# Attention halves of the third block emitted in 18 steps between linear matmuls, and spatial gating behind the second half's query, key and value linears

## The chip, the cores and the metric

The kernel runs on one core of a Trainium2 chip. The metric is the time of one execution on the device in microseconds (us), as the median of several runs. A second, separate execution is taken by the hardware profiler; its trace gives the durations of single instructions.

## The reference, cut to what matters

The model is three blocks in a row on 512 tokens of width 1024. The change touches the third block alone, between the normalisation of its input and the projection of its merged output:

```python
h = rms_norm_3(x, mix_norm[l])
z = h @ w_in[l]
g_a, g_b, z_uv, z_q, z_k, z_v = jnp.split(z, COL_SPLITS, axis=-1)
y_a = gmlp_chunk_mixer(z_uv, a_ln_gain[l], a_ln_bias[l], a_w_s[l], a_b_s[l])
...
y_b = diff_attention(q, k, v, positions, ...)
m = jax.nn.sigmoid(g_a) * (y_a @ a_w_proj[l]) + jax.nn.sigmoid(g_b) * (y_b @ b_w_proj[l])
x = x + m @ w_out[l]
```

The first branch is a gated mixer, the second a differential attention, in which each head subtracts one softmax from another:

```python
def gmlp_chunk_mixer(z_uv, ln_g, ln_b, w_s, b_s):
    z = jax.nn.gelu(z_uv, approximate=False)
    u, v = jnp.split(z, 2, axis=-1)
    v = layer_norm(v, ln_g, ln_b)
    vc = v.reshape(bsz, seq // CHUNK_3, CHUNK_3, A_GROUPS, A_GROUP_DIM)
    w = jnp.where(causal[None], w_s, jnp.zeros_like(w_s))
    f = jnp.einsum('gts,bcsge->bctge', w, vc) + b_s.T[:, :, None]
    return u * f.reshape(bsz, seq, A_WIDTH)

...
s = jnp.einsum('bhmqd,bhmkd->bhmqk', qb, kf)
p = jax.nn.softmax(jnp.where(mask, s, -jnp.inf), axis=-1)
a = p[:, :, 0] - lam * p[:, :, 1]
return jnp.einsum('bhqk,bhkd->bhqd', a, vf)
```

The last lines stand in `diff_attention`, behind the norm and the rotary turn of q and k; its output is normalised for each head after them.

## The kernel before

**Linears.** All activations stand in SBUF in tiles of 128 x 512. A linear is written as three matmuls for each product, high weight by high input, high weight by low input, low weight by high input. Weights come by DMA from the SP queue (line 236), ScalarE rounds them to the high part (line 218, `split`), VectorE subtracts that for the low part (line 219), 1024 columns at a time. `lin_fm` gives its output feature-major: matmuls of 512 columns (lines 248 to 250, called by line 261) into one bank. `lin_tm` gives it token-major: two halves of 256 output columns, each of 96 matmuls of 256 columns (lines 277 to 279) into two banks.

**PSUM banks.** The names of tiles in the trace tell the pool. `pl` has two banks and stays for the whole kernel (`ps_lin`). `pa` has two (`ps`), `pq` two pairs (`ps_pair`, the scores). `env.banks()` closes the pool of pa and pq and opens a new one. Line 269 toggles `self.bank` at each half of a `lin_tm`, and line 270 takes pa or pl by it.

**The third block.** Attention is done in two halves of four heads. The order in which the work is written is: query, key and value linears of the first half (`qk_half`, `v_half`); its attention `attend(0)`; the linear of u (feature-major, gelu in line 1885) and of v of the gating (token-major, gelu in line 1893 and a layer norm of each 128 tokens up to line 1905); the spatial gating (64 matmuls of line 1913, the gate in lines 1915 to 1918 and a split); `finish(o0)`, which turns the four outputs of the half (line 1858) and splits them; query, key and value of the second half; `attend(1)`; the gates of the first branch with their projections (`gated`, 288 matmuls in lines 248 to 250); `finish(o1)`; the gates of the second branch.

`qk_half` copies the linear's output, squares and sums it, applies the rotary turn (lines 1767 to 1772), takes a root (lines 204 to 213) and scales each 128 tokens (line 1778). Then 16 transposes by TensorE into four pa tiles (line 1783) and a copy of each by ScalarE (line 1785) turn it. `attend` has 16 heads' parts, one for each of four query tiles `b` and four heads. Each is a chain over four engines: scores in a pq pair (line 108), maximum and two exponentials (lines 1826 and 1827), reciprocal, scaling, subtraction, up to four transposes (line 1836), a copy, up to four product matmuls (line 1842) and a copy (line 1843). After four heads `safe_norm` normalises the output tile (up to line 1809).

**What sets the order.** Each engine runs its own queue strictly in order. A scheduler fixes these queues when the kernel is built: of the instructions that are ready by its cost model it takes the one written first, unless a priority is raised. So where attention is written ahead of a linear, the linear's matmuls fill what attention leaves, and what is written in a mixed order comes out mixed.

Of the kernel before, what the change touches and what calls it, by code (L numbers as in the profile page):

```python
# [17 lines left out]
ALU = mybir.AluOpType  # L18
PSUM = bass.MemoryType.PSUM

P = 128
S = 512
D = 1024
NC4 = S // P
# [9 lines left out]
class Env:  # L34
# [5 lines left out]
    def __init__(self, tc, ctx, n_long=33, n_tmp=6, n_scan=8, n_out=4):  # L40
# [12 lines left out]
        self.stream, self.bank = "", 0  # L53

# [197 lines left out]
    def lin_fm(self, w, c0, ncols, h, epi, k0=0, nk=KB, ready=()):  # L252
# [3 lines left out]
        for t in range(ncols // P):  # L256
            ps = self.ps_lin()
            for ka, kb in zip(cuts, cuts[1:]):
                wh, wl = ready[t] if t < len(ready) else self.weights(w, k0 + ka, kb - ka, c0 + t * P, P)
                for k in range(ka, kb):  # L260
                    self.mm3(ps, wh[:, k - ka, :], wl[:, k - ka, :], h[0][k], h[1][k], k == 0, k == nk - 1)
            epi(t, ps)

    def lin_tm(self, w, c0, h, epi, ncols=S):
# [3 lines left out]
        for g in range(ncols // n):  # L268
            self.bank = 1 - self.bank
            banks = [(self.ps, self.ps_lin)[self.bank]() for _ in range(2)]  # L270
            ps = [banks[c // 2][:, (c % 2) * n:(c % 2 + 1) * n] for c in range(NC4)]
            for ka in range(0, KB, 4):
                wh, wl = self.weights(w, ka, 4, c0 + g * n, n)
                for k in range(ka, ka + 4):
                    for c in range(NC4):
# [3 lines left out]
                        mm(ps[c], h[0][k][:, tok], wl[:, k - ka, :], start=False, stop=k == KB - 1 and c % 2 == 1)  # L279
            for c in range(NC4):  # L280
                epi(c, g, ps[c])
# [1379 lines left out]
def third_block(env, a, x):  # L1661
# [153 lines left out]
    def attend(half, qf, kf, vt):  # L1815

        outs = []

        def head(b, hd, o):
# [12 lines left out]
            nc.vector.scalar_tensor_tensor(ex[0][:, :n], ex[0][:, :n], st[:, 6:7], ex[1][:, :n], ALU.mult, ALU.subtract)  # L1832
            with env.on(""):
                ps = env.ps()
            for s in range(b + 1):
                nc.tensor.transpose(H(ps, s), H(ex[0], s), env.ident)  # L1836
            pt = env.tmp()
            nc.scalar.copy(pt[:, :n], ps[:, :n])
# [4 lines left out]
            nc.scalar.copy(H(o, hd), po[:, :P])  # L1843

        for b in range(NC4):
            o = env.out()
            for hd in range(4):
                with env.on("ab"[hd % 2]):
                    head(b, hd, o)
            safe_norm(o)  # L1850
            outs.append(o)
        return outs
# [25 lines left out]
    env.banks()  # L1878
# [28 lines left out]
    ya = ([], [])  # L1907
    for pair in range(4):
        ps = env.ps()
        for c in range(NC4):  # L1910
            for e in range(2):
                g = 2 * pair + e
                mm(ps[e * 64:(e + 1) * 64, c * P:(c + 1) * P], vg[c][:, g * 64:(g + 1) * 64], H(wt[g // 4], g % 4), start=True, stop=True)
        t = env.tmp()
        c4 = lambda v: v.rearrange("p (c i) -> p c i", c=4)
        nc.vector.tensor_tensor(c4(t), c4(ps), H(bs, pair)[:, None, :].to_broadcast([P, 4, P]), ALU.add)
        nc.vector.tensor_tensor(ut[pair], t, ut[pair], ALU.mult)
        hi, lo = env.parts(ut[pair])
        ya[0].append(hi)
        ya[1].append(lo)  # L1920

# [66 lines left out]
```

## Time and profile before

| | |
|---|---|
| median of 3 runs | 2968.88 us (2967.75 to 2970.56) |
| profiled execution | 2967.77 us, span 2966.0 us |
| TensorE (PE) busy | 2880.2 us, 97% |
| VectorE (DVE) busy | 1723.3 us, 58% |
| ScalarE (ACT) busy | 1107.8 us, 37% |
| mean granted TensorE clock | 0.987 |

PE is TensorE's matmuls, PEld its weight loads, DVE is VectorE, ACT is ScalarE, SP issues DMAs. The span is the time from the first to the last instruction in the trace, 1.8 us less than that execution's own time. Busy shares are means over the span: a stage can stand beside them that is quite different. A row of a timeline gives start, duration, engine, line, operation, output and inputs with sizes, how many alike, and in brackets how long the engine was idle before and for whom it waited. Matmuls overlap, so that the distance of two starts is the pace, not the duration. The granted clock is given as a share of 2.4 GHz.

### The profile page before, as it was taken

The numbers are of one execution on the slowest core, as the hardware profiler recorded it, in microseconds if no ns is written. First come the engines' busy times: TensorE is split into PE (matmuls) and PEld (weight loads), VectorE is DVE, ScalarE is ACT, GpSimd is POOL, SyncE is SP. The second block draws the span as 40 slices with busy tenths as digits, with TensorE's granted clock in tenths as the row PEclk, the third lists the DMA queues.
The fourth block names the chain that finished last, engine by engine and source line by source line (L and its number), as shares of the span: only waits on it lengthen the run. The fifth ranks groups of instructions, "written<-read, shape, count | busy, mean of one in ns | idle before, by whom it ended". The sixth has DMA issues, their size and how long they took to land. (4 is left out here: it accounts for less than half of the span.)

```text
span 2966.0 us, 38950 instructions
## 1 busy us (share of the span) xinstructions
PE 2880.2 (97%) x14919; PEld 2380.8 (80%) x14919; DVE 1723.3 (58%) x3936; ACT 1107.8 (37%) x2086; POOL 47.5 (2%) x99
## 2 busy tenths in 40 slices
PE   7999999999999999989999999999999999999999
PEld 5878888888788886777878878888887978878887
DVE  7787737655655357987653563433667573554333
ACT  5435424433322234322353342222455562332221
POOL 1000000000000000000000000000000000000000
PEclk8999999999999999989999999999999999999999
DMA  5222233233445332222113423333322214333332
GB/s 139 69 71 67 73 93 93 66 102 93 140 140 169 91 96 87 77 57 52 46 33 89 124 81 100 94 99 100 125 72 71 65 58 128 100 93 96 97 93 92
DMA packets 481642, 269.03 MB, mean 91 GB/s; under 512 B 30591, under 2 KB 469056, under 8 KB 481456
## 3 DMA queue, kind: packets, MB, share of 16 engines
q1 hardware_dynamic: 445104, 254.62, 29.7%
q10 hardware_dynamic: 34512, 10.49, 1.4%
q0 software_dynamic: 1840, 1.43, 0.6%
q8 instruction: 118, 1.93, 0.3%
q14 instruction: 68, 0.56, 0.1%
HBM read 252.20 MB, written 14.16 MB: 90 GB/s over the span
## 5 line engine op out<-in xcount | busy, mean ns | idle before, releaser
L218 ACT CAST wh<-wr 128x1024 fp32r<-128x1024 f32 (+3 forms) x447 | 454.4, 1017 | 1288.4 <-PE pl L249 901.7
L250 PE MATMUL pl<-h,wl 128*128 128x512 f32 x2216 | 876.8, 396 | 13.9 <-DVE wl L219 13.8
L248 PE MATMUL pl<-h,wh 128*128 128x512 f32 x2216 | 878.4, 396 | 6.3 <-ACT wh L218 4.2
L249 PE MATMUL pl<-h,wh 128*128 128x512 f32 x2216 | 874.9, 395 | 0.0
L219 DVE TENSOR_TENSOR wl<-wr,wh 128x1024 fp32r<-128x1024 f32 (+3 forms) x447 | 526.2, 1177 | 439.8 <-ACT wh L218 433.9
L250 PEld LDWEIGHTS pl<-h,wl 128*128 128x128 f32 x2216 | 419.4, 189 | 103.7 <-DVE wl L219 17.4
L248 PEld LDWEIGHTS pl<-h,wh 128*128 128x128 f32 x2216 | 419.7, 189 | 97.2 <-ACT wh L218 6.5
L249 PEld LDWEIGHTS pl<-h,wh 128*128 128x128 f32 x2216 | 419.3, 189 | 86.3 <-issue 3.4
L250 PE MATMUL pl<-long,wl 128*128 128x512 f32 x648 | 253.3, 391 | 0.0
L249 PE MATMUL pl<-long,wh 128*128 128x512 f32 x648 | 252.9, 390 | 0.3 <-DVE long L219 0.3
L248 PE MATMUL pl<-long,wh 128*128 128x512 f32 x648 | 252.8, 391 | 0.0
L590 DVE SCALAR_TENSOR_TENSOR long<-pl,long 128x512 f32<-128x512 f32 x72 | 49.8, 691 | 175.9 <-PE pl L250 175.9
L249 PEld LDWEIGHTS pl<-long,wh 128*128 128x128 f32 x648 | 121.7, 188 | 25.7 <-DVE long L219 0.7
L250 PEld LDWEIGHTS pl<-long,wl 128*128 128x128 f32 x648 | 121.7, 188 | 25.4 <-issue 0.8
L248 PEld LDWEIGHTS pl<-long,wh 128*128 128x128 f32 x648 | 121.7, 188 | 24.8
L578 DVE TENSOR_TENSOR tmp<-tmp,pl 128x512 f32<-128x512 f32 x66 | 45.4, 687 | 150.0 <-PE pl L250 150.0
L248 PE MATMUL pl<-tmpa,wh 128*128 128x512 f32 (+1 forms) x312 | 125.0, 401 | 4.8 <-DVE tmp L685 2.8
L249 PE MATMUL pl<-tmpb,wh 128*128 128x512 f32 (+1 forms) x312 | 124.6, 400 | 0.0
L250 PE MATMUL pl<-tmpa,wl 128*128 128x512 f32 (+1 forms) x312 | 124.0, 397 | 0.0
L248 PEld LDWEIGHTS pl<-tmpa,wh 128*128 128x128 f32 (+1 forms) x312 | 59.4, 191 | 18.7 <-ACT h L218 3.5
L250 PEld LDWEIGHTS pl<-tmpa,wl 128*128 128x128 f32 (+1 forms) x312 | 59.3, 190 | 13.8 <-issue 0.5
L249 PEld LDWEIGHTS pl<-tmpb,wh 128*128 128x128 f32 (+1 forms) x312 | 59.3, 190 | 12.7 <-issue 0.3
(781 smaller groups left out, 3947.7 us busy)
## 6 DMA issues: line engine op xcount, KB each, us to landing
wr<-in_w_in SPq DMA_DIRECT2D x169, 512.0 KB, 3.9
wr<-in_w_ffn_in SPq DMA_DIRECT2D x44, 512.0 KB, 3.9
wr<-in_ffn_w_gate SPq DMA_DIRECT2D x44, 512.0 KB, 3.8
wr<-in_ffn_w_up SPq DMA_DIRECT2D x44, 512.0 KB
wr<-in_ffn_w_down SPq DMA_DIRECT2D x32, 448.0 KB, 3.6
wr<-in_w_ada SPq DMA_DIRECT2D x24, 512.0 KB, 3.6
wr<-in_w_out SPq DMA_DIRECT2D x16, 512.0 KB, 4.1
wr<-in_ffn_w_down SPq DMA_DIRECT2D x16, 512.0 KB, 3.9
```

The costliest lines, as they stand in the source:

```text
L218: pin(self.nc.scalar.copy(hi, src))
L219: pin(self.nc.vector.tensor_tensor(lo, src, hi.bitcast(F32), ALU.subtract))
L248: mm(ps, wh, xh, start=first, stop=False)
L249: mm(ps, wh, xl, start=False, stop=False)
L250: mm(ps, wl, xh, start=False, stop=last)
L578: nc.vector.tensor_tensor(t1, t1, ps, ALU.mult)
L590: nc.vector.scalar_tensor_tensor(x[i], ps, scale, x[i], ALU.mult, ALU.add)
```

## The change

The 16 heads' parts of `attend` are cut in three works, `scores`, `turned` and `products`, and `attend` becomes a generator of 18 steps: step i emits the products of part i - 2, the transposes of part i - 1 and the scores of part i. The first step of a half is emitted at once. The others are called from inside linears: `env.weave(o0, 3)` hands the generator to `Env`, and `step` runs one of its steps after every three k steps of a `lin_fm` (nine matmuls), where a k step of a `lin_tm` (12 matmuls) counts as two. For the second half it is one step after every five k steps. `unweave` emits what is left. While a generator is handed over, `lin_tm` does not toggle the bank but holds it at 1 (pl). The first half is so emitted between the matmuls of u and v of the gating, the second between those of the first branch's gates and projections. The spatial gating and `finish` of the first half move behind the second half's query, key and value linears. No arithmetic changes.

```diff
@@ Env
+    def weave(self, side, every):
+        self.side, self.every, self.count = side, every, 0
+
+    def step(self, n=1):
+        self.count += n
+        if self.side is not None and self.count >= self.every:
+            self.count -= self.every
+            kept, self.stream = self.stream, ""
+            if next(self.side, self) is self:
+                self.side = None
+            self.stream = kept
+
+    def unweave(self):
+        for _ in self.side or ():
+            pass
+        self.side = None
@@ lin_fm
                     self.mm3(ps, wh[:, k - ka, :], wl[:, k - ka, :], h[0][k], h[1][k], k == 0, k == nk - 1)
+                    self.step()
@@ lin_tm
         for g in range(ncols // n):
-            self.bank = 1 - self.bank
+            self.bank = 1 - self.bank if self.side is None else 1
             banks = [(self.ps, self.ps_lin)[self.bank]() for _ in range(2)]
...
                         mm(ps[c], h[0][k][:, tok], wl[:, k - ka, :], start=False, stop=k == KB - 1 and c % 2 == 1)
+                    self.step(2)
@@ attend
-        def head(b, hd, o):
+        def scores(b, hd):
             n = (b + 1) * P
...
             nc.vector.scalar_tensor_tensor(ex[0][:, :n], ex[0][:, :n], st[:, 6:7], ex[1][:, :n], ALU.mult, ALU.subtract)
+            return ex[0]
+
+        def turned(b, ex):
             with env.on(""):
                 ps = env.ps()
             for s in range(b + 1):
-                nc.tensor.transpose(H(ps, s), H(ex[0], s), env.ident)
+                nc.tensor.transpose(H(ps, s), H(ex, s), env.ident)
             pt = env.tmp()
-            nc.scalar.copy(pt[:, :n], ps[:, :n])
+            nc.scalar.copy(pt[:, :(b + 1) * P], ps[:, :(b + 1) * P])
+            return pt
+
+        def products(b, hd, pt):
+            if hd == 0:
+                outs.append(env.out())
+            o = outs[b]
             with env.on(""):
                 po = env.ps()
             for s in range(b + 1):
                 mm(po[:, :P], H(pt, s), H(vt[s], hd), start=s == 0, stop=s == b)
             nc.scalar.copy(H(o, hd), po[:, :P])
-
-        for b in range(NC4):
-            o = env.out()
-            for hd in range(4):
-                with env.on("ab"[hd % 2]):
-                    head(b, hd, o)
-            safe_norm(o)
-            outs.append(o)
-        return outs
+            if hd == 3:
+                safe_norm(o)
+
+        heads = [(b, hd) for b in range(NC4) for hd in range(4)]
+        kept = {}
+        for i in range(len(heads) + 2):
+            for lag, work in ((2, products), (1, turned), (0, scores)):
+                j = i - lag
+                if 0 <= j < len(heads):
+                    b, hd = heads[j]
+                    with env.on("ab"[hd % 2]):
+                        if lag == 0:
+                            kept[j] = scores(b, hd)
+                        elif lag == 1:
+                            kept[j] = turned(b, kept[j])
+                        else:
+                            products(b, hd, kept.pop(j))
+            yield outs
@@ the order of the third block
     o0 = attend(0, qf, kf, vt)
-    env.banks()
+    a0 = next(o0)
+    env.weave(o0, 3)
...
     env.lin_tm(w_in, VG0, h, vg_epi)
-    ya = ([], [])
-    for pair in range(4):
...
+    env.unweave()
+    env.banks()
...
-    finish(o0)
     qf, kf, vt = qk_half(Q0 + S, 0), qk_half(K0 + S, 1), v_half(1)
+    ya = ([], [])
+    for pair in range(4):
...
+    finish(a0)
     env.banks()
     o1 = attend(1, qf, kf, vt)
+    a1 = next(o1)
+    env.weave(o1, 5)
+    gated(GA0, a["a_w_proj_3"][0], ya, 4, True)
+    env.unweave()
     env.banks()
-    gated(GA0, a["a_w_proj_3"][0], ya, 4, True)
-    finish(o1)
+    finish(a1)
     gated(GB0, a["b_w_proj_3"][0], yb, 8, False)
```

The change inserts lines above, so that line 1783 of before (the query's and key's transposes) is line 1806 after it, 1785 is 1808, 1778 is 1801, 277 to 279 are 299 to 301, 1893 is 1937, 1827 is 1852, 1913 is 1977. Two places show how it moves instructions.

The first place is TensorE's queue between the query and the key linear of the second half. `pa` and `pl` are banks, `h` is the input, `wh` and `wl` a weight's parts, `long` the scaled query. Before, at the first transposes of the query:

```order
L279 MATMUL pl_19807<-wl_19865,h_17578 128x256
L277 MATMUL pl_19807<-wh_19864,h_17578 128x256
L278 MATMUL pl_19807<-wh_19864,h_17579 128x256
L279 MATMUL pl_19807<-wl_19865,h_17578 128x256
L1783 MATMUL pa_19777<-ident_98,long_19530 128x128
L1783 MATMUL pa_19784<-ident_98,long_19530 128x128
L277 MATMUL pl_19806<-wh_19864,h_17584 128x256
L278 MATMUL pl_19806<-wh_19864,h_17585 128x256
L279 MATMUL pl_19806<-wl_19865,h_17584 128x256
L1783 MATMUL pa_19777<-ident_98,long_19545 128x128
```

After, first behind the query's last matmul:

```order
L300 MATMUL pl_19483<-wh_19540,h_17591 128x256
L301 MATMUL pl_19483<-wl_19541,h_17590 128x256
L1806 MATMUL pa_19669<-ident_98,long_19422 128x128
L1806 MATMUL pa_19676<-ident_98,long_19422 128x128
L1806 MATMUL pa_19669<-ident_98,long_19437 128x128
L1806 MATMUL pa_19676<-ident_98,long_19437 128x128
L1806 MATMUL pa_19669<-ident_98,long_19452 128x128
L1806 MATMUL pa_19676<-ident_98,long_19452 128x128
L1806 MATMUL pa_19669<-ident_98,long_19467 128x128
```

and at the key's first:

```order
L1806 MATMUL pa_19690<-ident_98,long_19422 128x128
L1806 MATMUL pa_19690<-ident_98,long_19437 128x128
L1806 MATMUL pa_19690<-ident_98,long_19452 128x128
L1806 MATMUL pa_19690<-ident_98,long_19467 128x128
L299 MATMUL pa_19698<-wh_19702,h_17548 128x256
L300 MATMUL pa_19698<-wh_19702,h_17549 128x256
L301 MATMUL pa_19698<-wl_19703,h_17548 128x256
```

Before, the key's matmuls into pl are already running when the first transposes come, and go on between them. After, the query's second half is in pl, its 16 transposes follow without anything between them, and the key's first matmul, now into a pa bank, comes behind the last of them; the same turn stands again between key and value.

The second place is ScalarE's queue in the v linear of the gating. `sums` and `junk` belong to the gelu with its sum and to the normalisation of an attention output, `tmpa` and `tmpb` are exponentials, `wh` is a weight's rounding. Before, from the first v gelu on:

```order
L218 CAST wh_19101<-wr_19099 128x1024
L1805 ACTIVATE junk_18780,s_18773<-out_18662 128x128 x4
L1893 ACTIVATE long_19089,sums_18978<-pl_18979 128x256
L1893 ACTIVATE long_19091,sums_18978<-pl_18979 128x256
L218 CAST wh_19155<-wr_19153 128x1024
L1893 ACTIVATE long_19093,sums_18978<-pl_18980 128x256
L1893 ACTIVATE long_19095,sums_18978<-pl_18980 128x256
L218 CAST wh_19424<-wr_19422 128x1024
L1893 ACTIVATE long_19089,sums_18978<-pa_19097 128x256
L1893 ACTIVATE long_19091,sums_18978<-pa_19097 128x256
```

After:

```order
L1866 COPY tmpa_18907<-pa_18902 128x512
L1937 ACT_TABLE_LOAD
L1937 ACTIVATE long_19045,sums_18756<-pl_18757 128x256
L1877 COPY out_18941<-pa_18942 128x128
L1828 ACTIVATE junk_18877,s_18870<-out_18722 128x128
L1852 ACT_TABLE_LOAD
L1852 ACTIVATE tmpa_18959,s_18955<-tmpa_18959,s_18955 128x512
L1828 ACTIVATE junk_18877,s_18870<-out_18722 128x128
L1852 ACTIVATE tmpa_18962,s_18955<-tmpa_18962,s_18955 128x512
L1828 ACTIVATE junk_18877,s_18870<-out_18722 128x128
L1937 ACT_TABLE_LOAD
L1937 ACTIVATE long_19047,sums_18756<-pl_18757 128x256
```

Before, the gelus of v stand behind all exponentials of the half, with only weight roundings and the last normalisation among them, and the second half's are in a pa bank. After, they stand among the exponentials, and each change from one function to the other has a table load, where before the last one of the half stands ahead of u's last gelu.

## Rows read from the trace of the kernel before

**Rows 1.** The page, section 1: engine, busy us, share of the span, instructions.
```profile
PE 2880.2 (97%) x14919; PEld 2380.8 (80%) x14919; DVE 1723.3 (58%) x3936; ACT 1107.8 (37%) x2086; POOL 47.5 (2%) x99
```

**Rows 2.** Windows of the third block: start:end, length, busy time by engine, clock, DMA.
```profile
2195.20:2250.00 54.80, 52.40 (x281) 34.50 (x280) 41.77 (x180) 51.28 (x149) 0.00 (x0) 1.00 0.13 40
2250.00:2274.40 24.40, 24.39 (x203) 23.95 (x202) 11.27 (x31) 10.30 (x29) 0.00 (x0) 1.00 0.36 109
2274.40:2300.40 26.00, 20.42 (x178) 18.23 (x177) 23.37 (x86) 10.70 (x25) 0.00 (x0) 0.93 0.20 61
2300.40:2363.40 63.00, 62.12 (x514) 61.23 (x513) 38.36 (x160) 28.28 (x62) 0.00 (x0) 1.00 0.22 68
2363.40:2419.00 55.60, 53.16 (x291) 35.97 (x290) 43.86 (x187) 46.56 (x149) 0.00 (x0) 1.00 0.14 41
2419.00:2460.90 41.90, 41.90 (x186) 34.63 (x185) 16.91 (x37) 12.38 (x24) 0.00 (x0) 1.00 0.34 99
```

**Rows 3.** Timeline of PE, query to key: start us, us, line, operation, idle before.
```profile
2311.97 0.28 PE L279 MATMUL pa<-wl,h 128*128 128x256 f32 x1
2312.09 0.28 PE L277 MATMUL pl<-wh,h 128*128 128x256 f32 x1
...
2321.33 0.44 PE L1783 MATMUL pa<-ident,long 128*128 128x128 f32 x2 [0.44 <-DVE long L1778]
...
2324.24 0.66 PE L1783 MATMUL pa<-ident,long 128*128 128x128 f32 x4
```

**Rows 4.** Timeline of PE, products and scores of a head, first attention half.
```profile
2209.24 0.67 PE L1842 MATMUL pa<-long,tmpa 128*128 128x128 f32 x4
2209.67 0.47 PE L250 MATMUL pl<-h,wl 128*128 128x512 f32 x1
2210.07 0.59 PE L108 MATMUL pq<-long,long 64*128 64x384 f32 x1
...
2210.50 0.48 PE L108 MATMUL pq<-long,long 64*128 64x384 f32 x1
```

**Rows 5.** Timeline of PE, the second half of the spatial gating.
```profile
2293.40 3.34 PE L1913 MATMUL pa<-long,long 128*64 128x128 f32 x32 [0.67 <-DVE tmp L1916]
```

**Rows 6.** Waits of PE, 2195 to 2461: who for whom, us, times, longest.
```profile
PE pa L1913 <- DVE long L1905: 3.3, 2, 2.9
```

**Rows 7.** Timeline of DVE, query to key.
```profile
2311.98 0.19 DVE L1767 TENSOR_TENSOR s<-long,turn 128x32 f32<-128x32 f32 x1 [2.50 <-ACT long L1759]
...
2315.11 1.22 DVE L219 TENSOR_TENSOR wl<-wr,wh 128x1024 fp32r<-128x1024 f32 x1
...
2319.45 1.23 DVE L219 TENSOR_TENSOR wl<-wr,wh 128x1024 fp32r<-128x1024 f32 x1
2320.59 2.49 DVE L1778 TENSOR_TENSOR long<-long,s 128x512 f32<-128x512 f32 x4
```

**Rows 8.** Timeline of ACT, query to key: copies of the turned tiles.
```profile
2324.94 1.27 ACT L1785 ACTIVATE long<-pa,gcol 128x512 f32<-128x512 f32 x2 [0.17 <-PE pa L1783]
```

**Rows 9.** Windows of an earlier stage, where TensorE stood (columns as in Rows 2).
```profile
1260.00:1271.00 11.00, 0.72 (x4) 0.00 (x0) 11.00 (x24) 0.70 (x2) 0.00 (x0) 0.64 0.11 27
...
1273.00:1280.00 7.00, 6.99 (x26) 5.89 (x27) 5.79 (x11) 1.31 (x4) 0.00 (x0) 0.50 0.60 155
1397.50:1401.50 4.00, 0.00 (x0) 0.00 (x0) 4.00 (x18) 0.00 (x0) 0.00 (x0) 0.75 0.08 8
1401.50:1406.00 4.50, 4.08 (x10) 3.21 (x11) 4.50 (x10) 0.00 (x0) 0.00 (x0) 0.50 0.69 177
```

**Rows 10.** Timeline of ACT, a table load in the first attention half.
```profile
2211.68 0.20 ACT L1827 ACTIVATION_READ_ACCUMULATOR tmpa<-tmpa,s 128x1 f32 x1
2211.89 1.28 ACT L1885 ACT_TABLE_LOAD   x1
2213.18 0.60 ACT L1885 ACTIVATE long<-pl 128x512 f32<-128x512 f32 x1
```

**Rows 11.** Timeline of ACT and DVE, the second half's last normalisation.
```profile
2418.46 0.27 ACT L1843 COPY out<-pa 128x128 f32<-128x128 f32 x1 [1.25 <-PE pa L1842]
...
2424.92 0.69 DVE L1809 TENSOR_TENSOR out<-out,s 128x512 f32<-128x512 f32 x1
```

More of the change, by code (lines that the diff above doesn't have):

```diff
@@ L53, in __init__ @@
         self.stream, self.bank = "", 0
+        self.side, self.every, self.count = None, 0, 0
+    def weave(self, side, every):
[12 more added lines that the diff above has]
+        self.side = None
     @contextmanager
@@ L1906, in third_block @@
     env.lin_tm(w_in, VG0, h, vg_epi)
-    ya = ([], [])
-    for pair in range(4):
[L1909 to L1920, printed above, removed]
+    env.unweave()
+    env.banks()
     merged = [None] * 8
@@ L1937, in gated @@
             env.lin_fm(wproj, t0 * P, P, y, proj_epi, nk=nk)
-    finish(o0)
     qf, kf, vt = qk_half(Q0 + S, 0), qk_half(K0 + S, 1), v_half(1)
+    ya = ([], [])
+    for pair in range(4):
+        ps = env.ps()
+        for c in range(NC4):
+            for e in range(2):
+                g = 2 * pair + e
+                mm(ps[e * 64:(e + 1) * 64, c * P:(c + 1) * P], vg[c][:, g * 64:(g + 1) * 64], H(wt[g // 4], g % 4), start=True, stop=True)
+        t = env.tmp()
+        c4 = lambda v: v.rearrange("p (c i) -> p c i", c=4)
+        nc.vector.tensor_tensor(c4(t), c4(ps), H(bs, pair)[:, None, :].to_broadcast([P, 4, P]), ALU.add)
+        nc.vector.tensor_tensor(ut[pair], t, ut[pair], ALU.mult)
+        hi, lo = env.parts(ut[pair])
+        ya[0].append(hi)
+        ya[1].append(lo)
+    finish(a0)
     env.banks()
     o1 = attend(1, qf, kf, vt)
+    a1 = next(o1)
+    env.weave(o1, 5)
+    gated(GA0, a["a_w_proj_3"][0], ya, 4, True)
+    env.unweave()
     env.banks()
-    gated(GA0, a["a_w_proj_3"][0], ya, 4, True)
-    finish(o1)
+    finish(a1)
     gated(GB0, a["b_w_proj_3"][0], yb, 8, False)
```

## The prediction

> **What bounds the kernel now.** I read the page first: TensorE is busy 97% of the span, ScalarE 37% [rows 1]. So the time moves only where TensorE stands or is slowed, and the question is how much of that lies in the part of the third block that the change rewrites. The table by stage answers it [rows 2]. Its last row gives the pace without trouble: 186 matmuls in 41.9 us, 0.225 us for one of 512 columns (lines 248 to 250). One of 256 columns (lines 277 to 279) starts 0.12 us after the other [rows 3], so half a token-major linear, 96 of them, is 11.5 us.
>
> Against this pace the stages hold so much:
> - 2195.2 to 2274.4, the first attention half beside u and v of the gating: 96 x 0.225 + 192 x 0.12 = 44.6 us of linears. One attention half has 40 transposes and 80 product passes at 0.11 (four start in 0.43), 13.2 us, and 32 score passes; a pass of 384 columns takes 0.43, and the way into it 0.40 where a linear matmul has 0.225 [rows 4]. Over the four sizes and some 13 groups I estimate 13 us for the scores, 26.2 for a half. With 0.9 for the turned gating weights that is 71.7 in 79.2 us: 7.5 lost.
> - 2274.4 to 2300.4: 11.5 of the query linear, 4.3 of gating (estimated: 32 of its 64 passes take 3.3, mostly at half clock [rows 5]) and 1.8 for 16 transposes, 17.6 in 26.0: 8.4 lost, 3.3 of it in waits for the layer norm's last line [rows 6].
> - 2300.4 to 2363.4: five half linears and 32 transposes, 57.6 + 3.5 = 61.1 in 63.0: 1.9 lost.
> - 2363.4 to 2460.9, the second half beside the gates: 288 x 0.225 + 26.2 = 91.0 in 97.5: 6.5 lost.
>
> All that the change can win is thus about 24 us.
>
> **The turn from query to key, the largest term.** Before, every token-major linear puts its first 256 columns in the pl banks and its second in the pa banks. The query's turning (line 1783) takes pa banks, and the key's first half meanwhile runs in pl: in the order before, the transposes stand among the key's matmuls. Now line 291 holds the bank at 1 during the v linear, so the toggle comes out one step further on: query, key and value of the second half begin in pa and end in pl. The key's first half needs the same two pa banks as the turning, and on TensorE all 16 transposes stand between the query's last matmul and the key's first. Nothing else is queued there, and the queue runs in order.
>
> What TensorE will wait for can be read off now. The query's last matmul starts at 2311.97 and the first transpose at 2321.33: 9.24 us after that matmul's slot, covered so far by 72 key matmuls [rows 3]. VectorE fills this time with rotary, sums and root, then four scalings that begin at 2320.59; two weight subtractions of 1.23 lie among them, one just ahead of the scalings [rows 7]. In the new order that one comes behind the scalings, so I take 8.0. From the first transpose to the third tile's (2324.24) and its copy, the first of two that take 1.27 from 2324.94, another 4.2 us pass [rows 3, 8]; then the key's first bank is free. So TensorE goes 12.2 us between linears and does 16 x 0.11 = 1.8 of work: 10.4 lost. The turn from key to value is the same: twice, 20.8 us. Bounds: 9.2 each if neither subtraction is in the way, 11.6 if both are.
>
> The clock adds to that. After 11 us from 1260 in which TensorE was busy for 0.72, its granted clock was 0.50 (1.2 of 2.4 GHz) through 7 us of dense work from 1273, and 0.50 again through 4.5 us of work behind 4 us in which it did nothing [rows 9]. Here it stands 8 us and then turns 16 sparse tiles. I take 4.6 us of linears at half clock, 2.3 lost each time; ends 0 and 3.5. The old loss of this stretch, 1.9, goes. Sum: 20.8 + 4.6 - 1.9 = +23.5 (ends +16.5 and +28.3).
>
> **Gating behind the linears.** The layer norm's wait goes, and with it the 8.4. What is late next: VectorE's 12 operations for the gate and four for the turned attention output, queued ahead of the first scores' reductions. Over them stand the gating itself and 24 gate matmuls (5.4 us). I take 2.0 left, ends 0 and 5: -6.4.
>
> **First attention half between u and v.** TensorE could go down to its 71.7 (-7.5). But ScalarE is busy 51.28 of the first 54.80 us and 61.6 over the stage [rows 2], and each gelu of u and of v's first half now falls among exponentials: up to there the order of ScalarE has 13 table loads where it had 7. A load takes 1.28 [rows 10]: 7.7 more. 69.3 at the present share of 0.94 is 74.0, and 2.5 us of linear remain behind it. The place where it is paid is the v linear: both its halves are in pl now, so the second waits for the four gelus of the first, which stand among three table loads and two long exponentials, some 9 us of ScalarE work over 3 to 4 of matmuls. The high end is all six loads uncovered, +7.7. I take 77.0, by ScalarE: -2.2.
>
> The rows price a switch at the load alone: the activation starts 1.29 us after the load starts, and the load 0.01 after the end of what is before it [rows 10]. The Trainium skill (ScalarE: Activation LUTs, section "What ACT_TABLE_LOAD costs") gives 1283 ns and a drain of 1380 ns besides, 2.66 us for a switch. By it the six would cost ScalarE 16.0 us, and the sum would come out up to 8.3 higher. The trace agrees with the load and shows no drain.
>
> **Second attention half in the gate stage.** Five steps, 15 matmuls of 0.225, now lie between two heads: 3.4 us and the head's own 1.6 for a chain of two reductions, two exponentials, a scaling and a combination. ScalarE gets 97.5 us for its 58.9 of work, where 46.56 of that fell in the first 55.60 [rows 2], so most waits go. The score groups rise from 27 to 31 over both halves; at 0.3 each (0.1 in each of two passes, and up to 0.17 going in) [rows 4] this half pays 0.6. I take 3.0 of its 6.5 as left: -2.9 (ends -5.9 and +2). At its end 33 matmuls (7.4 us) cover the last normalisation, 7.2 us from 2418.46 to the end of line 1809 [rows 11]: nothing, or 1.2 if a weight subtraction slips in.
>
> **The sum.** 23.5 - 6.4 - 2.2 - 2.9 = +12.0. The profiled execution took 2967.77 (span 2966.0), which gives 2979.8; the median of the runs is 1.1 higher: 2981 us. The linears and their weight transfers keep their number; only their place changes.
>
> **Rivals.**
> - A, not slower: the spread halves lose nothing any more. Place: the u and v stage and the gate stage, from -2.2 and -2.9 to their ends -7.5 and -5.9. The sum is then 23.5 - 6.4 - 13.4 = +3.7, 2972.6, which can't be told from no change. For it: ScalarE is the one crowded engine there and gets 30% more room. Against it: six more table loads in the first half. It decides from the point where the first half takes under 73 us.
> - B, ScalarE sets both halves: the six loads are uncovered (+7.7 for -2.2) and the gate stage gains nothing: +12.0 + 9.9 + 2.9 = +24.8, 2994. For it: the 94%. Against it: v's matmuls have few exponentials over them.
> - C, cheap turns: the chain runs without either subtraction and the clock stays at full: +16.5 in place of +23.5, +5.0, 2974. For it: nothing else is asked of VectorE then. Against it: VectorE is full from 2311.98 on [rows 7], and both stands in [rows 9] were followed by half clock.
> - D, the transposes find other banks and the turns stay covered: the order excludes it.
>
> **Chances.** The forecast, turns paid and a part won back (2975 to 2990): 0.68. A 0.10, C 0.09, both together (-3.3, about 2966) 0.03, B 0.09, D 0.01. A measurement of this kernel can tell about 0.2%, 5.9 us: A, C and both lie within it for the most part, D below it. So faster 0.03, same 0.19, slower 0.78. The range takes in the lower part of A and B's value: 2971 to 2994.
>
> **What would show it.** Two gaps of TensorE of 10 to 13 us, some 35 us apart, ended by line 1801 on VectorE and then by line 1808 on ScalarE, with a granted clock of 0.5 in them or behind; none over 1 us at the gating (line 1977); ScalarE above 90% while u is computed, and a wait of v's second half for line 1937. If the turns lose less than 8 us each, the largest step is wrong; if it takes over 82 us from the first matmul of u to the query's first, that of the first half.

## The result, and the profile after

The changed kernel takes 2989.56 us (median of 4 runs, 2987.8 to 2990.55) against 2968.71 (2967.75 to 2970.56): ratio 1.0064, 95% interval 1.0052 to 1.0076, 20.9 us slower. The profiled execution took 2990.55 us, its span is 2988.8. In the changed code the linears are lines 269 to 271 and 299 to 301, the weights' rounding and subtraction 239 and 240, the query's and key's scaling, transposes and copy 1801, 1806 and 1808, exponentials 1852, the heads' transposes 1864, v's gelu 1937, the gating 1977.

The page's busy times, as in [rows 1], barely move; ScalarE has 10.3 us more:

```profile
PE 2886.8 (97%) x14919; PEld 2387.9 (80%) x14919; DVE 1723.6 (58%) x3936; ACT 1118.1 (37%) x2092; POOL 47.4 (2%) x99
```

The windows of the third block after the change, columns as in [rows 2]: the stage of u, v and the first half; the query's linear; the turn to the key; the key's first half; the turn to the value; its first half; the gating; the gate stage.

```profile
2194.09:2278.79 84.70, 78.66 (x482) 60.78 (x481) 50.92 (x195) 69.19 (x175) 0.00 (x0) 0.98 0.18 54
2278.80:2301.80 23.00, 23.00 (x194) 22.99 (x192) 21.77 (x121) 11.96 (x36) 0.00 (x0) 1.00 0.22 69
2301.80:2315.00 13.20, 4.58 (x19) 2.73 (x17) 9.66 (x46) 4.82 (x11) 0.00 (x0) 0.65 0.26 81
2315.00:2328.40 13.40, 13.40 (x97) 13.40 (x97) 1.23 (x1) 2.16 (x4) 0.00 (x0) 0.84 0.12 39
2339.90:2353.20 13.30, 4.68 (x20) 2.82 (x18) 9.74 (x46) 4.90 (x11) 0.00 (x0) 0.62 0.14 40
2353.20:2366.40 13.20, 13.20 (x97) 13.20 (x97) 1.22 (x1) 2.25 (x4) 0.00 (x0) 0.86 0.07 21
2377.80:2386.70 8.90, 8.79 (x94) 7.07 (x93) 7.43 (x12) 4.85 (x10) 0.00 (x0) 1.00 0.20 59
2386.70:2481.90 95.20, 92.61 (x464) 69.94 (x463) 63.78 (x226) 62.90 (x175) 0.00 (x0) 1.00 0.21 62
```

The reader is to see two things. In the turns TensorE is busy 4.6 of 13.2 us, and the granted clock is 0.65 and 0.62 there and 0.84 and 0.86 behind. And the first stage takes 84.7 us, where TensorE's work did not grow but ScalarE's did.

The waits of TensorE from 2190 to 2490 (who for whom, us, times, longest):

```profile
PE pa L1806 <- DVE long L1801: 16.1, 2, 8.1
PE pl L299 <- ACT long L1937: 4.5, 1, 4.5
...
PE pa L1806 <- ACT long L1808: 1.1, 2, 0.6
```

The layer norm's 3.3 us of [rows 6] are gone; two waits of 8.1 and one of 4.5 stand in their place. The first turn in TensorE's timeline, which answers to [rows 3]:

```profile
2301.71 0.28 PE L301 MATMUL pl<-wl,h 128*128 128x256 f32 x1
2310.05 2.49 PE L1806 MATMUL pa<-ident,long 128*128 128x128 f32 x8 [8.06 <-DVE long L1801]
2313.11 1.97 PE L1806 MATMUL pa<-ident,long 128*128 128x128 f32 x8 [0.56 <-ACT long L1808]
2315.00 0.58 PE L299 MATMUL pa<-wh,h 128*128 128x256 f32 x1
```

From the query's last matmul to the key's first it is 13.29 us, where [rows 3] had 0.12; the second turn takes 13.28 (2339.90 to 2353.18).

**Stages of all kernels.** The starts are read from TensorE's timeline: the first matmul of u's stage, the query's first, the second half's first score, the first transpose of that half's output, and the first gate matmul behind its sixteen transposes; the last 2.6 to 3.0 us are in the sum alone. The stages are those of the one profiled execution of each kernel. Median beside that of the kernel before in the same runs.

| kernel | median, before (us) | ratio, 95% interval | u, v, first half | query to gating | gates, second half | sum |
|---|---|---|---|---|---|---|
| before | | | 79.24 | 90.51 | 95.94 | 268.34 |
| changed | 2989.56, 2968.71 | 1.0064 [1.0052, 1.0076] | 84.71 | 109.25 | 93.90 | 290.86 |
| e1_parity | 2972.69, 2969.03 | 1.0017 [1.0008, 1.0026] | 85.54 | 89.83 | 93.77 | 272.14 |
| e2_before_flip | 2991.97, 2969.03 | 1.0082 [1.0068, 1.0096] | 80.03 | 112.23 | 99.15 | 294.05 |
| e3_no_weave0 | 2982.94, 2969.03 | 1.0050 [1.0035, 1.0066] | 95.15 | 89.34 | 93.72 | 281.20 |
| e4_gating_only | 2965.31, 2969.03 | 0.9990 [0.9980, 1.0000] | 79.95 | 87.51 | 95.11 | 265.22 |
| e5_weave1_gating | 2965.80, 2969.22 | 0.9988 [0.9979, 0.9996] | 80.03 | 89.06 | 94.12 | 266.20 |
| e6_no_gelu_v | 2985.86, 2969.22 | 1.0051 [1.0037, 1.0065] | 78.94 | 109.07 | 93.25 | 284.25 |
| e7_gelus_together | 2993.86, 2969.22 | 1.0078 [1.0066, 1.0091] | 85.72 | 109.28 | 93.87 | 291.85 |
| e8_norm_behind_q | 2964.13, 2969.22 | 0.9984 [0.9974, 0.9993] | 80.06 | 85.86 | 94.12 | 263.05 |
| e9_busy_gap | 2991.52, 2969.76 | 1.0073 [1.0061, 1.0086] | 85.03 | 106.68 | 93.85 | 288.55 |
| e10_no_steps | 2964.49, 2969.76 | 0.9982 [0.9973, 0.9992] | 79.47 | 85.85 | 95.18 | 263.16 |
| e11_every4 | 2990.60, 2968.97 | 1.0065 [1.0049, 1.0081] | 80.10 | 113.80 | 93.86 | 290.74 |
| e12_all_mended | 2963.02, 2968.97 | 0.9978 [0.9968, 0.9989] | 78.71 | 86.84 | 93.74 | 262.28 |

The change costs 22.5 us in this stretch (290.86 - 268.34): +5.5, +18.7, -2.0 and +0.3.

These differences mix loss with work that has changed its stage. Behind the value linear, the first matmuls of the gates (lines 269 to 271) now stand among the gating (1977) and the turning of the first output (1902), ahead of the second half's first score (129):

```profile
2378.01 3.18 PE L1977 MATMUL pa<-long,long 128*64 128x128 f32 x48
2381.12 0.50 PE L269 MATMUL pl<-h,wh 128*128 128x512 f32 x1
...
2381.78 1.09 PE L1977 MATMUL pa<-long,long 128*64 128x128 f32 x16
2382.80 0.66 PE L1902 MATMUL pa<-ident,out 128*128 128x128 f32 x4
...
2386.71 0.48 PE L271 MATMUL pl<-h,wl 128*128 128x512 f32 x1
...
2388.05 0.37 PE L129 MATMUL pq<-long,long 64*128 64x128 f32 x1
```

Of the 288 gate matmuls, 6 stand ahead of that score before the change and 16 behind it. Ten of them are 2.3 us at 0.225, which the middle stage has more and the gate stage less. So by work the change is +5.5, +16.5, +0.2 and +0.3: the gate stage won nothing. The count is 16 in e6, e7, e9 and e11 too, 0 in e2 and 19 in the others.

### The profile page after: what moved, and what is told of

It is laid out like the page before. It is cut to its first block, busy times and chain, and to the rows that moved or that the text cites. A ratio compares the mean times of both kernels' runs of the same rounds, so it can differ in the third digit from the quotient of the medians.

```text
span 2988.8 us, 38929 instructions
## 1 busy us (share of the span) xinstructions
PE 2886.8 (97%) x14919; PEld 2387.9 (80%) x14919; DVE 1723.6 (58%) x3936; ACT 1118.1 (37%) x2092; POOL 47.4 (2%) x99
## 5 line engine op out<-in xcount | busy, mean ns | idle before, releaser
L271 PE MATMUL pl<-h,wl 128*128 128x512 f32 x2216 | 876.5, 396 | 12.9 <-DVE wl L240 12.7
L299 PE MATMUL pl<-wh,h 128*128 128x256 f32 x256 | 74.5, 292 | 4.5 <-ACT long L1937 4.5
L301 PE MATMUL pl<-wl,h 128*128 128x256 f32 x256 | 74.2, 290 | 0.0
L300 PE MATMUL pl<-wh,h 128*128 128x256 f32 x256 | 73.9, 289 | 0.0
```

Of the source, the lines that this page charges most:

```text
L271: mm(ps, wl, xh, start=False, stop=last)
L299: mm(ps[c], h[0][k][:, tok], wh[:, k - ka, :], start=k == 0 and c % 2 == 0, stop=False)
L300: mm(ps[c], h[1][k][:, tok], wh[:, k - ka, :], start=False, stop=False)
```

## The experiments

**e1_parity: the bank set back.**

```diff
+    env.bank = 0
     qf, kf, vt = qk_half(Q0 + S, 0), qk_half(K0 + S, 1), v_half(1)
```

> The changed kernel with one line more: the bank is set so that query, key and value of the second half begin in pl and end in pa, as before the change; all else as changed. Theory (the two turns cost 13.3 us each between linears only because the key's, and then the value's, first half has no bank until the turning is done): both waits of TensorE for the scaled query and key (8.1 us each) go, with them some 4 us of half clock, and the old loss of about 2 us in this stretch comes back; about 25 us less than the changed kernel, 2965 us (2962 to 2969), faster than before. Rival (VectorE's chain is what is late, whatever the bank): TensorE stands about as long in another place, 2980 us or more.

Measured: 2972.69 us, 17 below the changed kernel in place of 25. The turns are covered again, and the waits for the scaling are 0.9 us in all. Its waits of TensorE from 2190 to 2470:

```profile
PE pl L299 <- ACT long L1937: 5.0, 2, 4.5
...
PE pa L301 <- DVE wl L240: 1.8, 1, 1.8
...
PE pa L1806 <- DVE long L1801: 0.9, 2, 0.4
```

The new row is the middle one: the query's second half waits for low weights. Its windows, as in [rows 2]:

```profile
2296.80:2300.10 3.30, 1.00 (x7) 0.59 (x5) 3.30 (x16) 0.75 (x1) 0.00 (x0) 1.00 0.00 0
2300.10:2306.90 6.80, 6.78 (x44) 6.79 (x45) 1.33 (x4) 0.43 (x2) 0.00 (x0) 0.75 0.51 157
```

TensorE does seven matmuls in 3.3 us, and the 44 behind take 6.8 us at a clock of 0.75, 1.5 more than 44 x 0.12. So the theory on the turns holds and its size does not: part of what was to come back is lost to a wait in another place.

**e2_before_flip: the turns alone.**

```diff
-    qf, kf, vt = qk_half(Q0 + S, 0), qk_half(K0 + S, 1), v_half(1)
+    qf = qk_half(Q0 + S, 0)
+    env.bank = 1
+    kf, vt = qk_half(K0 + S, 1), v_half(1)
```

> The kernel before with one edit: the key's linear of the second half begins in pa instead of pl, and so does the value's. Theory: the two turns alone cost what they cost in the changed kernel, 23 to 27 us more than before (about 2993 us), with two waits of some 8 us for the scaled query and key ahead of the transposes and a granted clock of about 0.65 over the gap and behind it. Rival (the price in the changed kernel comes partly from what was moved beside it, the gating above all): less than 15 us more.

Measured: 22.9 us more than before, as the theory has it. Its waits of TensorE from 2190 to 2490 begin with

```profile
PE pa L1783 <- DVE long L1778: 16.2, 2, 8.1
```

the same two waits of 8.1 us, without any attention in steps and with the gating in its old place. The stage of the query to the gating is 21.7 us longer, 23.1 by work, as it has six gate matmuls fewer. Of the 3.2 us that the gate stage is longer, 1.4 are these six; the rest was not followed up.

**e3_no_weave0: the first half in one piece, in the new order.**

```diff
-    env.weave(o0, 3)
+    for _ in o0:
+        pass
+    env.banks()
...
     env.lin_tm(w_in, VG0, h, vg_epi)
-    env.unweave()
-    env.banks()
```

> The changed kernel with the first attention half written in one piece ahead of u and v, as before; the gating is still moved and the second half still in steps, and v's halves toggle again, so that the turns are covered. Theory (the first half's steps cost 5.5 us of the change, the turns 25, the gating wins 6 and the second half 2): 2961 us (2958 to 2964), and 79 us from u's first matmul to the query's first. Rival (the stage of u and v is slower for another reason than the steps, the query's first half being pulled into it or the 18-step order itself): that stage stays at 83 us or more, and the time at 2965 or more.

Measured: 2982.94 us; the first stage takes 95.15 us. The theory falls for this kernel: it is not the half as it was before. Written 18 steps in a row, where the products of a head come two scores later, the scheduler lets v's gelus stand among the exponentials all the same, and the last heads come late. The largest of its waits of TensorE between 2205 and 2301 is one for a head's combination:

```profile
PE pa L1864 <- DVE tmpb L1857: 9.2, 4, 6.5
```

The first half by heads is e4's and e5's.

**e4_gating_only: the gating alone**, as in the last part of the change's diff, without steps.

> The kernel before with the spatial gating and the turning of the first attention output moved behind the second half's query, key and value linears, and nothing else of the change. Theory (the wait for the layer norm goes and about 2.4 us are lost at the new place): 6 us less than before, 2963 us (2960 to 2965). Rival (what is won is given back in front of the second half's scores, because VectorE and ScalarE have the gate, the split and the key's and value's ends to do there): no change, 2967 to 2970 us.

Measured: 3.7 us less than before, where 6 were expected. By the table the middle stage is 3.0 us shorter; it does 13 gate matmuls more (2.9 us), so by work it wins 5.9, and the gate stage, which has them less, loses 2.1. Where this second loss stands was not looked for. In the middle stage a loss stands where neither the theory nor the rival put it: in this kernel too the query's second half has a gap, 2.66 us between starts at 2299.04 and 2301.70. ScalarE's timeline ahead of it (line 1902 is the layer norm's square, 1759 the query's copy, 218 the rounding):

```profile
2288.89 0.63 ACT L1902 ACTIVATE tmp<-long 128x512 f32<-128x512 f32 x1 [0.60 <-DVE s L211]
...
2292.21 0.63 ACT L1902 ACTIVATE tmp<-long 128x512 f32<-128x512 f32 x1 [2.60 <-DVE long L1900]
...
2292.84 0.63 ACT L1759 COPY long<-pl 128x256 f32<-128x256 f32 x2
...
2295.12 1.06 ACT L218 CAST wh<-wr 128x1024 fp32r<-128x1024 f32 x1
```

The last square waits 2.6 us for VectorE, which works at four layer norms, and the query's copies and the next rounding stand behind it in the queue.

**e5_weave1_gating: e4 with the second half in steps.** The first half is written with the `attend` of before (here `attend_whole`):

```diff
-    o0 = attend(0, qf, kf, vt)
-    a0 = next(o0)
-    env.weave(o0, 3)
+    a0 = attend_whole(0, qf, kf, vt)
+    env.banks()
```

> The changed kernel with the first attention half as it was before the change (head by head, ahead of u and v, banks as before), the gating moved, and the second half in 18 steps among the gates. Beside e4_gating_only it shows the second half's steps alone, beside e1_parity the first half's. Theory (the second half's steps win about 1.5 to 2 us; the first half's steps cost 6): 1.5 to 2 us below e4_gating_only, about 4.5 us below the kernel before (2964.5 us), with 79 to 80 us from the first matmul of u's stage to the query's first and 95.5 us in the gate stage. Rival (the gate stage was only shorter because the first half had been served earlier): 97 us in the gate stage and no gain over e4_gating_only.

Measured: no gain over e4 that the runs can tell (0.9988 and 0.9990). The gate stage is 1.0 us shorter than in e4, and the last transposes give 0.3 back; in the middle stage the gap in the query was followed by a granted clock of 0.76 for 7 us, in e4 by 1.00. The steps of the second half are worth under 1 us.

**e6_no_gelu_v: six table loads fewer.**

```diff
-        nc.scalar.activation(vg[c][...], ps, AF.Gelu, accum_out=...)
+        nc.scalar.activation(vg[c][...], ps, AF.Square, accum_out=...)
```

> The changed kernel with v's gelu replaced by a square, so that its result leaves out that gelu: six table loads of ScalarE fewer (17 for 23), and the scheduler then puts the four activations of v's first half pairwise side by side. Theory (the loads cost the first half its time): the stage from u to the query's first matmul falls from 84.7 to about 78 us, the time to 2983 us. Rival (only the wait of v's second half for a gelu that stands behind two exponentials costs, 4.8 us and the clock behind it): 79 to 80 us, 2984.5. Taken alone these two can't be told apart; it is the bound for e7_gelus_together.

Measured: the first stage takes 78.94 us, 5.8 less than the changed kernel's. Its window, as in [rows 2]:

```profile
2198.24:2277.18 78.94, 77.12 (x482) 59.35 (x481) 50.32 (x193) 62.74 (x170) 0.00 (x0) 1.00 0.19 58
```

ScalarE has 62.74 us of work where the changed kernel has 69.19. The 6.5 us of difference are less than six loads of 1.28 [rows 10]. The Trainium skill (ScalarE: Activation LUTs, "What ACT_TABLE_LOAD costs") gives 2.66 us for a switch with its drain, by estimate 16 us for six. No run here shows that drain. Without the loads the first half in steps is only 0.3 us better than before the change. As the gelus of v also stand pairwise here, this run does not tell loads from position.

**e7_gelus_together: steps held back.**

```diff
-                    self.step(2)
+                    if k < KB - 4:
+                        self.step(2)
             for c in range(NC4):
                 epi(c, g, ps[c])
+            for _ in range(4):
+                self.step(2)
```

> The changed kernel with the attention steps of the last four of the eight k steps of each half of v moved behind that half's four gelus. In ScalarE's queue the four gelus of v's first half then stand side by side, with the same 23 table loads. Theory (position: the bank that v's second half waits for is held by a gelu behind exponentials): the wait of 4.8 us is gone or under 1.5, the stage from u to the query's first matmul takes 79 to 81 us in place of 84.7, the time falls by 4 to 5 us to about 2985. Rival (the table loads: ScalarE has too much to do): the wait moves to another instruction of the stage, which stays at 83 us or more, and the time within 2 us of the changed kernel's 2989.6.

Measured: 2993.86 us and 85.72 in the first stage; as the rival has it, the wait moved. Its largest wait of TensorE from 2190 to 2280 now stands ahead of a last head's transposes (line 1867 of this kernel):

```profile
PE pa L1867 <- DVE s L233: 4.0, 1, 4.0
```

The row names a root of the layer norm (line 233). What the transposes read is the head's combination (line 1860, 2274.32 to 2275.07), and its exponentials stand behind a table load at 2270.06. As the steps held back make the last heads late by themselves, this run does not tell loads from position. e11 comes nearer.

**e8_norm_behind_q: e5 with the layer norm behind the query's linear.** The lines of `vg_epi` from the sum on become `vg_norm(c)`:

```diff
+    qf = qk_half(Q0 + S, 0)
+    for c in range(NC4):
+        vg_norm(c)
+    kf, vt = qk_half(K0 + S, 1), v_half(1)
```

> e5_weave1_gating with the layer norm of the gating's v written behind the query's linear instead of inside v's. Theory (what the moved gating still loses is the query's second half, which waited 2.7 to 3.3 us in e4_gating_only and e1_parity for low weights, because four layer norms stand ahead of its weights' rounding in ScalarE's and VectorE's queues): that wait goes, 3 to 4 us less than e5_weave1_gating, about 2961 us, faster than both kernels. Rival (VectorE has the layer norms to do anyway and they only move in front of the key's turning, whose scaling comes later): the query's or the key's turn loses as much, and the time stays within 1 us of e5_weave1_gating.

Measured: 2964.13 us; the middle stage takes 85.86, 3.2 us less than in e5, and the stretch from u to the gates 263.05, 5.3 less than before. By the medians it is 1.7 below e5, within what the intervals leave open; the stage shows the wait gone.

**e9_busy_gap: TensorE kept at work in the turns.**

```diff
+        if col0 in (Q0 + S, K0 + S):
+            fill = env.ps_pair()[0]
+            for _ in range(34):
+                mm(fill, h[0][0][:, :P], h[0][1], start=True, stop=True)
         r = env.rsqrt(ss, 32, 1.0 / 64, 1e-6)
```

> The changed kernel with 34 matmuls of 512 columns into a score bank that nobody reads, written behind the query's and again behind the key's linear of the second half; 33 of each stand in TensorE's queue between the linear's last matmul and the first transpose, 7.4 us in a gap of 8.3. No other work is added or left out. Theory (some 4 us of the turns' price are the lower clock behind the gap): the key's and the value's first 96 matmuls take 11.5 us each in place of 13.4 and 13.1, the granted clock behind the turns is 1.00, and the time falls by 3 to 4 us to about 2986. Rival (the sixteen sparse transposes lower the clock by themselves, or the gap's price is waiting alone): 13 us each as before, and no gain.

Measured: 2991.52 us, no gain by the medians. The matmuls that nobody reads (line 1802) did not come out alike in the two turns. In the first, 34 filled the gap and nine more, of those written for the second, stood among the transposes. In the second, 24 were left, TensorE still stood 2.6 us, and the transposes (line 1810) had none among them:

```profile
2306.42 7.89 PE L1802 MATMUL pq<-h,h 128*128 128x512 f32 x34
...
2342.11 5.63 PE L1802 MATMUL pq<-h,h 128*128 128x512 f32 x24
2350.32 0.44 PE L1810 MATMUL pa<-ident,long 128*128 128x128 f32 x2 [2.58 <-DVE long L1805]
```

The first turn and the key's first half, as in [rows 2]:

```profile
2306.40:2319.00 12.60, 12.28 (x62) 9.40 (x60) 9.64 (x46) 4.90 (x12) 0.00 (x0) 1.00 0.27 83
2319.00:2330.50 11.50, 11.50 (x97) 11.50 (x97) 1.22 (x1) 2.08 (x4) 0.00 (x0) 1.00 0.15 47
```

The clock stays at 1.00, and the key's first half takes 11.6 us (2318.98 to 2330.59) in place of 13.5. Behind the second turn the value's first half took 12.9. The middle stage is 2.6 us shorter than the changed kernel's: in this trace the clock is part of the price, 1.9 us in the turn that was filled. The medians don't show it. Whether the sparse transposes lower the clock by themselves stays open, as they were alone in no turn without a stand before them.

**e10_no_steps: e8 without any step.** The second half, too, is `attend_whole`, ahead of the gates.

> e8_norm_behind_q with the second attention half as before the change too, so that nothing is left of the 18 steps: the gating and the first output's turning behind the second half's linears, and the layer norm behind the query's. Theory (the steps of the second half win under 1 us net, as e5_weave1_gating beside e4_gating_only shows): within 1 us of e8_norm_behind_q, about 2964 us, with 97 us in the gate stage in place of 95.9. Rival (with the layer norm out of the way the steps have more room): 2 us or more above e8_norm_behind_q.

Measured: 2964.49 us, and 263.16 where e8 has 263.05. So the gain of e8 shows without any step: it is that of the gating's and the layer norm's place.

**e11_every4: another pace.**

```diff
-    env.weave(o0, 3)
+    env.weave(o0, 4)
```

> The changed kernel with one number changed: the first half's steps come after every four k steps of the linear instead of three. The four gelus of v's first half then stand side by side in ScalarE's queue, as in e7_gelus_together, but no step is held back; 21 table loads in place of 23. Theory (position): the wait of 4.8 us in v's second half goes, and the stage from u to the query's first matmul takes 80 to 81 us in place of 84.7; the time falls by some 4 us to about 2985.5. Rival (the loads by their number: six of them cost 5.8 us in e6_no_gelu_v, so two give back 1.9): 82.7 us and about 2987.5. A third (the last heads come later with four than with three, as the held-back steps did in e7_gelus_together): 85 us or more, the wait standing before the last transposes.

Measured: the first stage takes 80.10 us, as the theory of position has it, with 21 loads; the wait for the gelu is gone. The time stays at 2990.6: the middle stage is 4.6 us longer than the changed kernel's, as the query now has the gap of e1 and e4. Of its waits of TensorE from 2285 to 2302 there is one:

```profile
PE pl L301 <- DVE wl L240: 2.7, 1, 2.7
```

The query's last 96 matmuls take 15.8 us (2284.96 to 2300.79) in place of 11.4.

**e12_all_mended: e8 with the first half in steps too**, `env.weave(o0, 4)` and `env.bank = 0` behind v.

> e8_norm_behind_q with the first half in steps as well, after every four k steps, and the bank set so that the turns stay covered: all of the change, with the turns mended and the layer norm behind the query's linear. Theory: what e11_every4 shows for the stage of u and v decides; at 80 us the time is that of e8_norm_behind_q within 1 us, about 2964, and below it only if the stage takes less than 79. Rival (the first half's steps cost in any form): 85 us in that stage and 2969, no better than the kernel before.

Measured: 2963.02 us, 0.9978 of before (0.9968 to 0.9989), 6 us faster than the kernel before and 26.5 below the changed one's median. The first stage takes 78.71, the rival's 85 does not come. e8, e10 and e12 lie within each other's intervals, so no gain of the steps is shown.

## Why the prediction was right, and where it was not

It said slower, 2981 us in a range of 2971 to 2994; it came out at 2989.56. By the profiled executions the forecast was +12.0 and the stretch from u to the gates lost 22.5. It is right by its largest term, the turns; the two attention halves, which were to win 5.1 together, lost 6.0, and the gating won 1.7 more than forecast.

**The turns and the clock, +23.5: right, a little low.** Two gaps, ended by the scaling (line 1801) and then by the copy (line 1808). Each has 13.29 us between linears, where 12.2 were worked out; less 1.8 of work and 0.1 of pace, 11.4 are lost in place of 10.4. The wait ahead of the transposes was 8.2 for 8.0, with one weight subtraction in the chain (at 2304.84), as taken; from the first transpose to the key it took 4.95 for 4.2, at a granted clock of 0.50. The half linears behind take 13.5 and 13.2 us in place of 11.4 or 11.5, so the clock costs 2.0 and 1.7 where 2.3 were taken. With the 1.9 us of old loss that go, this is 24.6; e2 measured 22.9 by the medians with nothing else changed. The order of TensorE was enough to see it, and rival D was rightly excluded.

**The gating, -6.4: right in kind, -8.1 measured.** The middle stage changed by +16.5 by work; less the turns' 24.6 the gating won 8.1. From the value's last matmul to the gate matmul at 2386.71 it is 8.8 us, but 4.1 of these are gating, 1.8 transposes and 2.5 eleven gate matmuls: some 0.4 are lost where 2.0 were taken.

That it came out so is luck in one place. The step's question, what is late next, has another answer in e4, e1 and e11: the layer norm takes ScalarE and VectorE from the query's second half, which then has a gap (none in e8, which moves it). In the changed kernel ScalarE rounds the weights that this half needs (line 239) ahead of the layer norm's last square (line 1946), and VectorE subtracts (line 240) at once, as the two engines' timelines show:

```profile
2290.43 1.05 ACT L239 CAST wh<-wr 128x1024 fp32r<-128x1024 f32 x1
2291.39 0.36 ACT L1782 COPY long<-pa 128x256 f32<-128x256 f32 x1
2291.65 0.64 ACT L1946 ACTIVATE tmp<-long 128x512 f32<-128x512 f32 x1
...
2291.55 1.22 DVE L240 TENSOR_TENSOR wl<-wr,wh 128x1024 fp32r<-128x1024 f32 x1
```

In e1, whose first stage is as late (85.54), the square stands at 2290.62, the rounding behind it at 2293.53 and the subtraction at 2298.85, when TensorE already waits. So it is the order of the queues that kept the gap away, and nothing in the prediction says which order would come out.

**The first attention half, -2.2: wrong by 7.7, and the largest miss.** The failing step is "69.3 at the present share of 0.94 is 74.0". The work was right: ScalarE is busy 69.19 us. The share was not: 69.19 of 84.70 is 0.82, and in e11, without the wait, 67.78 of 80.09 is 0.85. The 0.94 came from a window in which the heads were written ahead of u and v; in steps they come at the linear's pace, and ScalarE is never full. The first two parts of the stage, as in [rows 2]:

```profile
2194.10:2225.00 30.90, 30.74 (x155) 21.11 (x153) 18.82 (x80) 25.28 (x68) 0.00 (x0) 1.00 0.26 75
2225.00:2250.00 25.00, 23.90 (x156) 17.68 (x154) 16.16 (x64) 21.55 (x56) 0.00 (x0) 1.00 0.15 47
```

The shares are 0.82 and 0.86. The place of the loss was named rightly, and it is in ScalarE's timeline behind them:

```profile
2253.36 1.28 ACT L1937 ACT_TABLE_LOAD   x1
2254.66 0.38 ACT L1937 ACTIVATE long<-pl 128x256 f32<-128x256 f32 x1
...
2255.80 1.28 ACT L1852 ACT_TABLE_LOAD   x1
2257.09 0.72 ACT L1852 ACTIVATE tmpa<-tmpa,s 128x512 f32<-128x512 f32 x1
...
2258.10 0.70 ACT L1852 ACTIVATE tmpa<-tmpa,s 128x512 f32<-128x512 f32 x1
...
2259.21 1.28 ACT L1937 ACT_TABLE_LOAD   x1
2260.50 0.38 ACT L1937 ACTIVATE long<-pl 128x256 f32<-128x256 f32 x1
```

Two gelus empty one bank, and two exponentials and two loads lie between them: 5.8 us in which v's second half has no bank. TensorE stands 4.5 us, and the matmuls behind start 0.21 us apart for 3.5 us in place of 0.12, which loses 1.5 more. Without these 6.0 the stage would be at 78.7. The prediction names this very wait, 9 us of ScalarE over 3 to 4 of matmuls, but the sum has only ScalarE's work in it and not the wait. What of this is loads and what is position: e11 puts the gelus together with two loads fewer and gets 4.6 us back; e6 takes six loads away and gets 5.8. So most of the miss is the place of single gelus among exponentials. That two loads alone would not have done it follows only by the numbers (2.6 us of ScalarE), and e11 moves every other step as well. That the bank held at pl makes the place count is argued: no run has the first half in steps with v's second half in pa.

**The second half, -2.9: wrong, +0.5 by work** (+0.2 and +0.3). The step that failed is "so most waits go". TensorE is idle for 2.6 us of this stage (95.20 - 92.61), before for 2.4 [rows 2]. The stage is 2.0 us shorter only because ten gate matmuls left it. Beside the same order without steps (e5 and e4, e8 and e10) the steps win 1.0 in the stage and give 0.3 back, under what a measurement can tell.

**Rivals.** A's end for the first half (71.7) was never near: e12, with all mended, has 78.7. B comes nearest by the sum (+24.8), and both its parts are near: +5.5 in the first half for +7.7, and no gain in the gate stage. Its reason is not borne out: ScalarE is busy 0.82 and 0.66 of the two stages (69.19 of 84.70, 62.90 of 95.20), and what stands out in the first is one wait, the one that e11 took away. C did not come: a subtraction stood in the chain and the clock fell. Of the things to look for, ScalarE above 90% in u's stage failed; the stage's 84.7 us passed the 82 that was to show this step wrong.

## What to carry to other kernels

When a toggle chooses between two pools of PSUM banks, any change that holds or skips it once also shifts it for all that comes behind: look in the order of the engine for a stretch where the next linear and the work beside it ask for the same bank. A stage's share of a busy engine can't be carried into a new order: here, in steps, the heads came at the pace of the linear, and what cost most was which single instruction held a bank, not how much work there was. When work is moved from a wait, ask for each engine that it used what now stands behind it, for the wait that goes and also for the one that was hidden. When stages of two orders are compared, count the work between their boundaries first: ten gate matmuls made a stage look 2 us better that had won nothing.

## What the runs showed of the hardware

A stand of 8.2 us between dense linears, with sixteen transposes behind it, was followed by a granted clock of 0.84 and 0.86 over the next 96 matmuls, at a cost of 2.0 and 1.7 us. With 34 matmuls that nobody reads in the gap and nine among the transposes (e9, first turn) the clock stayed at 1.00 and the next 96 matmuls took 11.6 us; with 24 in the gap and a stand of 2.6 us (second turn) they took 12.9. A table load goes straight on into its activation (2253.36 to 2254.66, 1.30 us).
